# A forgetting attention inside a three-layer kernel: masked terms from GpSimd, outputs turned by transposes, second products in one PSUM bank

## The chip, the cores and the metric

The kernel runs on one core of a Trainium2 chip, as one program and one launch. The metric is the device time of an execution in microseconds (us). The core has five engines that each work through their own list of instructions in order and meet at semaphores: TensorE (PE; its weight loads are shown as PEld), VectorE (DVE), ScalarE (ACT), GpSimd (POOL) and SyncE (SP, which here issues the DMAs). Matmuls and transposes of PE write to PSUM, which has eight banks of 512 fp32 columns; DVE and ACT read it, and GpSimd does not touch it in this kernel.

## The reference, cut to what matters

The whole program is three layers: a first block with attention and experts, a second layer with "forgetting" attention, and a third with windowed attention. Only the forgetting attention is touched. Per head (16 heads of width 64, 1024 positions) it computes

```python
c = jnp.cumsum(log_f, axis=1)                       # one forgetting sum per position and head
logits = einsum('bqhd,bkhd->bhqk', q_block, k) * scale
logits = logits + c_q[..., :, None] - c_k[..., None, :]
logits = where(k_pos <= q_pos, logits, -inf)        # causal
p = softmax(logits)
out_block = einsum('bhqk,bkhd->bqhd', p, v)         # 8 blocks of 128 queries
```

The term of the query is the same along a row of the softmax and drops out; the kernel adds only the term of the key.

## The kernel before, in words

The instructions stand in the order in which the Python code emits them; semaphores between the engines are added for every true dependence. `phase_fox` runs 16 heads of 8 units, one unit for each block `qt` of 128 queries, in the order 7, 0, 6, 1, 5, 2, 4, 3 within a head (units 0 to 127 in all). A unit has n = (qt+1)*128 keys and passes four stages, each emitted while later units pass their earlier ones:

- **First products** (lines 2040, 2041): q times the two parts of k, in pieces of 512 columns, into banks 0 and 1 (even places in the order) or bank 2 (odd places). A third matmul of 128 columns (line 2042) adds the causal mask `cm` to the diagonal block. Then DVE (line 2047) subtracts the products from the forgetting row `c`, writes the result to SBUF and takes the minimum of each row.
- **Exponential** one unit later (line 2051, ACT).
- **Transposes** three units later (line 2066, PE, up to four blocks to a bank of `p_tr`: banks 4, 5, 6). `split` makes two parts of each: ACT copies the bank (line 341, the high part), DVE subtracts (line 342, the low part).
- **Second products** `pv_chunks` (lines 1993, 1994): v times both parts, for a pair of query blocks with the higher one called `top` (7, 1, 5, 3), 256 columns, in pieces of two key blocks that wait in the list `todo` and are emitted two to a unit ahead of the unit's first products. ACT copies the finished sum to `OT` (`acopy`, line 315).

The second products and the folds take their PSUM from one ring of two banks, 3 and 7 (`p_pv`). When a head is done, `fold_chunks` multiplies `OT` with a 128x64 matrix `fold` (line 2013, eight fp32 matmuls), which adds the two halves and turns the output at once; DVE divides by the row sums (line 2016, four instructions) and writes the outputs `og`.

`fox_load(h+1)` loads q, k and then `c` for the next head. The table `WO_FOX` puts work for the output weights beside chosen units: at units 119 to 122 GpSimd splits a quarter of a weight each time (lines 344 and 335 through `split`). GpSimd has no other work in this stage.

Of the kernel before, what the change touches and what calls it, by code (L numbers as in the profile page):

```python
# [124 lines left out]
def view(t, shape, dtype, o):  # L125
    n = math.prod(shape[1:])
    ap = t[:shape[0], o:o + n]
    if dtype is not t.dtype:
        ap = ap.bitcast(dtype)
    if len(shape) > 2:  # L130
        names = "abcd"[:len(shape) - 1]
        ap = ap.rearrange(f"p ({' '.join(names)}) -> p {' '.join(names)}", **dict(zip(names, shape[1:])))
    return ap
# [160 lines left out]
def three_layer_kernel(ctx: ExitStack, tc: tile.TileContext, I, out, stop=99, dbg=None):  # L294
    nc = tc.nc
    V, A, G, T, SP = (GUARD(e) for e in (nc.vector, nc.scalar, nc.gpsimd, nc.tensor, nc.sync))
    ctx.enter_context(tc.manual_schedule())
    sb = Arena(ctx.enter_context(tc.tile_pool(name="sbuf", bufs=1)), SLOTS, SMALL)
    banks = Banks(ctx.enter_context(tc.tile_pool(name="psum", bufs=1, space=PSUM)).tile([P, 4096], F32, name="ps"))
    p_mm = banks.ring([0], [1], [2], [3])  # L300
    p_s = banks.ring([0, 1], [2, 3])
    p_tr = banks.ring([4], [5], [6])
# [25 lines left out]
    def bc_load(dst, src_row, n):  # L328
        SP.dma_start(out=dst, in_=bass.AP(tensor=src_row.tensor, offset=src_row.offset,
                                          ap=[[0, dst.shape[0]], [1, n]]))  # L330
# [49 lines left out]
    def head_loads(dst, src, h, flip=False):  # L380

        for x in range(2):
            d, s = dst[x * 64:(x + 1) * 64], src[:, 1 - x if flip else x, h // 2]
            if len(dst.shape) == 2:
                SP.dma_start(out=f(d), in_=s[h % 2 * 64:(h % 2 + 1) * 64])
            else:
                SP.dma_start(out=f(d), in_=s.rearrange("(a p) n -> p a n", a=2))
# [1350 lines left out]
    FX = {}  # L1738

    def fox_load(h):  # L1740
        if h >= 16:
            return
        q = sb.tile([P, S], F32R, f"fq{h}")
        k = sb.tile([P, 2, S], F32R, f"fk{h}")
        c = sb.tile([P, S], F32, f"fc{h}")
        head_loads(q, d_aq, h)
        for x in range(2):
            head_loads(k[:, x], d_ak, h, x == 1)
        bc_load(c, d_c[h], S)
# [211 lines left out]

    def phase_fox(og, wo, last):

        p_s0, p_s1, p_pv = banks.ring([0, 1]), banks.ring([2]), banks.ring([3], [7])
        fc, pp, ptp, sm, ob = Rings(sb), Rings(sb, 2), Rings(sb, 2), Rings(sb, 4), Rings(sb, 2)
        cm, idr = fc.tile([P, P], F32R, name="cm"), fc.tile([P, P], F32R, name="idr")
        cmf = fc.tile([P, P], F32, name="cmf")
        V.memset(cmf, 0.0)
        G.affine_select(out=cmf, in_=cmf, compare_op=OP.is_ge, fill=-BIG, base=0, pattern=[[-1, P]],
                        channel_multiplier=1)  # L1970
        V.tensor_copy(cm, cmf)
        V.tensor_copy(idr, ident)
        fc.drop("cmf")
        pp.reserve_pairs("sb", 2)
        pp.reserve_pairs("pt", 4)
        OT, RS, PT = {}, {}, {}
        todo = Todo(FDELAY)


        ORDER = ((7, 0, 6, 1), (5, 2, 4, 3))  # L1980

        def pv_chunks(h, top, hi, lo):

            v = FX[h][3]
            box = {}

            def chunk(k0, k1):
                if k0 == 0:
                    box["ps"] = p_pv.tile([P, 256], name="pv")
                ps = box["ps"]  # L1990
                for kt in range(k0, k1):
                    q0 = P if kt == top else 0
                    T.matmul(ps[:, q0:], lhsT=v[:, kt], rhs=hi[:, kt, q0:], start=(kt == 0), stop=False)
                    T.matmul(ps[:, q0:], lhsT=v[:, kt], rhs=lo[:, kt, q0:], start=False, stop=(kt == top))
                if k1 == top + 1:
                    acopy(OT[h][:, (top - 1) * P:(top + 1) * P], ps)
                    if top == 3:
                        sb.drop(f"fv{h}")
                        fold_chunks(h)

            for k0 in range(0, top + 1, 2):
                todo.add(lambda k0=k0: chunk(k0, k0 + 2))

        def fold_chunks(h):
            box = {}

            def chunk(t0, t1):
                if t0 == 0:
                    box["po"] = p_pv.tile([P, NT, 64], name="po")
                    V.reciprocal(RS[h], RS[h])  # L2010
                po = box["po"]
                for t in range(t0, t1):
                    T.matmul(po[:, t], lhsT=OT[h][:, t * P:(t + 1) * P], rhs=fold, start=True, stop=True)
                if t1 == NT:
                    for t in range(0, NT, 2):
                        V.tensor_tensor(og[t // 2][:, :, h * 64:(h + 1) * 64], po[:, t:t + 2],
                                        RS[h][:, t:t + 2, None].to_broadcast([P, 2, 64]), op=OP.mult)

            for t0 in range(0, NT, 2):
                todo.add(lambda t0=t0: chunk(t0, t0 + 2))  # L2020

        def unit(h, half, i):
            todo.step()
            qt = ORDER[half][i]
            if half == 0 and i == 0:
                OT[h] = ob.tile([P, S], F32, name="ot", bufs=3)
                RS[h] = sm.tile([P, NT], F32, name="rs")
            if half == 0 and i == 3:
                fox_load(h + 1)
            if half == 1 and i == 2:  # L2030
                fox_load_v(h + 1)
            q, k, c = FX[h][:3]
            qs = slice(qt * P, (qt + 1) * P)
            n = (qt + 1) * P
            todo.some(FTAKE)
            ps = (p_s1 if i % 2 else p_s0).tile([P, 512 if i % 2 else S], name="s")
            for c0 in range(0, n, 512):
                w = min(512, n - c0)
                end = c0 + w == n
                T.matmul(ps[:, c0:c0 + w], lhsT=q[:, qs], rhs=k[:, 0, c0:c0 + w], start=True, stop=False)  # L2040
                T.matmul(ps[:, c0:c0 + w], lhsT=q[:, qs], rhs=k[:, 1, c0:c0 + w], start=False, stop=not end)
            T.matmul(ps[:, qs], lhsT=idr, rhs=cm, start=False, stop=True)  # L2042
            nm = sm.tile([P, 1], F32, name="nm")
            sbt = pp.tile([P, S], F32, name="sb")
            pt = pp.tile([P, S], F32, name="pt", bufs=4)

            V.tensor_tensor_reduce(sbt[:, :n], ps[:, :n], c[:, :n], -1.0, 3e38, OP.add, OP.min, nm)  # L2047
            if half == 1 and i == 3:
                sb.drop(f"fq{h}", f"fk{h}", f"fc{h}")
            yield  # L2050
            A.activation(out=pt[:, :n], in_=sbt[:, :n], func=AF.Exp, scale=-1.0, bias=nm,  # L2051
                         accum_out=RS[h][:, qt:qt + 1])
            yield
            yield
            kind = i % 2
            if i < 2:
                nb = (8, 4)[kind]
                PT[h, half, kind] = (ptp.tile([P, nb, 256], F32R, name=f"phi{kind}"),
                                     ptp.tile([P, nb, 256], F32R, name=f"plo{kind}"))
            hi, lo = PT[h, half, kind]  # L2060
            cs = slice((qt % 2) * P, (qt % 2 + 1) * P)
            for b in range(0, qt + 1, 4):
                m = min(4, qt + 1 - b)
                tr = p_tr.tile([P, 4, P], name="ptr")
                for j in range(m):
                    T.transpose(tr[:, j], pt[:, (b + j) * P:(b + j + 1) * P], ident)  # L2066
                split(hi[:, b:b + m, cs], lo[:, b:b + m, cs], tr[:, :m])
            if i >= 2:
                pv_chunks(h, qt | 1, hi, lo)

        for h in range(16):
            for half in range(2):
                for i in range(4):
                    wo.step(WO_FOX.get(8 * h + 4 * half + i, ()))
                    go.feed(unit(h, half, i))
        last()
        n = 0
        while go.active or go.fresh or not todo.empty():
            todo.step()
            todo.some(3)  # L2080
            go.feed()
            if n == 0:
                pp.drop("sb")
            if n == 2:
                pp.drop("pt")
            wo.step(WO_FOX.get(128 + n, ()))
            n += 1
        for r in (fc, pp, ptp, sm, ob):
            r.close()

    def new_og():
        return [sb.tile([P, 2, D], F32, f"og{q}") for q in range(4)]
# [294 lines left out]
```

## Time and profile before

| | |
|---|---|
| time, median of 3 runs | 2597.66 us (2596.23 to 2602.85) |
| the profiled execution | 2597.42 us, span 2595.7 us |
| share of the span, PE, PEld, DVE, ACT, POOL | 95%, 79%, 69%, 56%, 21% |
| the forgetting attention | about 1764.7 to 2016 us of the span |
| PE busy in 1780 to 1995 us | 214.78 of 215.00 us |

An engine's busy time counts its instructions from start to end; two that overlap count once. On PE the ends are modelled, so the distance from one start to the next says what an instruction costs there. In brackets behind an instruction stand its engine's idle time before it and the instruction that ended the wait.

### The profile page before, as it was taken

How to read it: one execution, taken by the hardware profiler on the slowest of the kernel's cores; microseconds unless marked ns; L12 is line 12 of the kernel's file. 1: busy time of each engine (PE TensorE's matmuls, PEld its weight loads, DVE VectorE, ACT ScalarE, POOL GpSimd, SP SyncE). 2: the span in 40 equal slices, each digit the busy share in tenths (PEclk: the TensorE clock that was granted, in tenths of full speed). 3: DMA queues.
4: the chain of work that ended last, by engine and by line, in shares of the span. 5: the costliest groups of instructions: out<-in, count | busy, mean ns of one | idle time of the engine just before them, and what ended most of it. 6: DMA issues, size and time to landing. Idle time of an engine off the chain costs nothing. (4 is left out here: it accounts for less than half of the span.)

```text
span 2595.7 us, 37353 instructions
## 1 busy us (share of the span) xinstructions
PE 2461.7 (95%) x13658; PEld 2053.3 (79%) x13658; DVE 1798.1 (69%) x3072; ACT 1458.0 (56%) x2557; POOL 557.7 (21%) x523
## 2 busy tenths in 40 slices
PE   5999899998988999999997999999999899999999
PEld 3789788887876777777765887899999789888977
DVE  7654588887668999999998354536888436735952
ACT  3324577777217878878874343436888224435930
POOL 0000089936002222222211012310002002300400
PEclk8999999999989999999998999999999899999999
DMA  7355765553748999999968524337667324338523
GB/s 267 114 140 164 231 195 162 172 185 110 255 162 307 384 390 386 385 380 382 381 245 315 166 89 147 112 111 198 165 171 204 114 85 147 118 110 190 148 73 106
DMA packets 270416, 530.04 MB, mean 204 GB/s; under 512 B 28027, under 2 KB 180603, under 8 KB 244118
## 3 DMA queue, kind: packets, MB, share of 16 engines
q1 hardware_dynamic: 263062, 510.84, 60.0%
q0 software_dynamic: 7168, 16.79, 1.9%
q8 instruction: 109, 1.79, 0.3%
q14 instruction: 77, 0.63, 0.1%
HBM read 424.19 MB, written 111.76 MB: 206 GB/s over the span
## 5 line engine op out<-in xcount | busy, mean ns | idle before, releaser
L365 PE MATMUL ps<-t,t 128*128 128x512 f32 (+5 forms) x8224 | 1758.3, 370 | 3.8 <-DVE t L342 2.4
L365 PEld LDWEIGHTS ps<-t,t 128*128 128x128 f32 (+1 forms) x8224 | 1377.0, 182 | 313.0 <-DVE t L342 4.4
L342 DVE TENSOR_TENSOR t<-t,t 128x2048 fp32r<-128x2048 f32 (+4 forms) x226 | 472.3, 2115 | 55.3 <-ACT t L341 55.2
L341 ACT ACTIVATE t<-ps 128x512 fp32r<-128x512 f32 (+3 forms) x660 | 334.2, 544 | 313.9 <-PE ps L377 205.1
L342 DVE TENSOR_TENSOR t<-ps,t 128x512 fp32r<-128x512 f32 (+3 forms) x660 | 391.8, 623 | 89.7 <-ACT t L341 83.2
L341 ACT ACTIVATE t<-t 128x2048 fp32r<-128x2048 f32 (+4 forms) x226 | 399.9, 1773 | 31.0 <-DVE t L774 10.9
L322 POOL TENSOR_TENSOR small<-small 128x8 f32<-128x8 f32 (+3 forms) x120 | 137.3, 1145 | 944.8 <-DVE small L321 912.2
L317 ACT ACTIVATE t<-ps,small 96x512 f32<-96x512 f32 (+5 forms) x208 | 128.6, 618 | 322.8 <-PE ps L365 278.0
L335 POOL TENSOR_TENSOR t<-t,t 128x256 f32<-128x256 f32 (+1 forms) x224 | 166.3, 774 | 27.1 <-DMA t<-in_b_ada_dram 23.3
L315 ACT ACTIVATE t<-ps 128x256 f32<-128x256 f32 (+4 forms) x196 | 88.4, 453 | 125.0 <-PE ps L365 69.9
L377 PE MATMUL ps<-small,t 96*128 96x96 f32 (+1 forms) x736 | 94.3, 267 | 47.4 <-DMA t<-d_ye 18.0
L1512 POOL DMA_INDIRECT d_ye<-t,small x32 | 45.2, 1413 | 435.7 <-ACT t L317 429.1
L377 PEld LDWEIGHTS ps<-small,t 96*128 96x128 f32 (+1 forms) x736 | 82.4, 145 | 68.1 <-DVE t L1880 18.5
L2129 DVE TENSOR_TENSOR t<-t,ps 128x512 f32<-128x512 f32 x32 | 22.0, 688 | 125.8 <-PE ps L365 125.8
L2047 DVE CUSTOM_DVE_ANT_0 t<-ps,t 128x1024 f32<-128x1024 f32 (+7 forms) x128 | 95.5, 747 | 19.5 <-PE ps L2042 17.6
L349 DVE SCALAR_TENSOR_TENSOR t<-t,small,t 128x512 fp32r<-128x512 f32 (+5 forms) x124 | 80.2, 692 | 35.7 <-ACT t L348 35.7
L2051 ACT ACTIVATE t<-t,small 128x1024 f32<-128x1024 f32 (+7 forms) x128 | 99.3, 776 | 7.7 <-DVE small L2047 5.4
L626 POOL TENSOR_SCALAR t<-t,small 128x1024 f32<-128x1024 f32 x32 | 92.6, 2894 | 31.9 <-DMA t<-in_w_ada_dram 31.9
L1508 POOL DMA_INDIRECT t<-d_h,small x32 | 89.0, 2781 | 37.5 <-DVE small L1216 28.0
L1090 PE MATMUL ps<-t,t 128*128 128x512 f32 x320 | 83.6, 408 | 8.1 <-ACT t L1136 7.6
L1709 DVE TENSOR_REDUCE small<-t 128x8 f32<-128x512 f32 (+1 forms) x56 | 36.2, 647 | 79.0 <-ACT t L1708 79.0
L2066 PE MATMUL ps<-small,t 128*128 128x128 f32 x576 | 86.2, 277 | 0.4 <-ACT t L2051 0.3
(296 smaller groups left out, 2966.9 us busy)
## 6 DMA issues: line engine op xcount, KB each, us to landing
t<-in_w_expert_gate_dram SPq DMA_DIRECT2D x64, 1024.0 KB, 11.6
t<-in_w_expert_up_dram SPq DMA_DIRECT2D x64, 1024.0 KB, 11.1
t<-in_w_expert_down_dram SPq DMA_DIRECT2D x64, 1024.0 KB, 10.5
t<-in_w_ada_dram SPq DMA_DIRECT2D x48, 512.0 KB, 5.2
t<-d_ak SPq DMA_DIRECT2D x64, 256.0 KB, 4.7
t<-in_w_in_a_dram SPq DMA_DIRECT2D x12, 1024.0 KB, 9.1
t<-in_x_dram SPq DMA_DIRECT2D x16, 512.0 KB, 5.4
t<-d_dk SPq DMA_DIRECT2D x16, 512.0 KB, 8.7
```

The source lines that it names most:

```text
L315: A.activation(out=dst, in_=src, func=AF.Copy)
L317: A.activation(out=dst, in_=src, func=AF.Copy, scale=scale)
L322: G.tensor_tensor(dst, dst, mhalf[:, :dst.shape[-1]], op=OP.pow)
L335: G.tensor_tensor(out[:, c:c + 256], a[:, c:c + 256], b[:, c:c + 256], op=op)
L341: A.activation(out=hi, in_=src, func=AF.Copy)
L342: e.tensor_tensor(lo, src, f(hi), op=OP.subtract)
L365: T.matmul(ps, lhsT=a(k), rhs=b(k), start=(first and i == 0), stop=(last and i == n - 1))
L377: T.transpose(ps[:, k], src[:, (c + k) * P:(c + k + 1) * P], ident[:m, :m])
L626: G.tensor_scalar(w, w, cc[:, k:k + 1], None, op0=OP.mult)
L1508: G.indirect_dma_start(out=xg[e % 3], out_offset=None, in_=d_h2, in_offset=rows(idx_in[:CAP, e:e + 1]), bounds_check=S - 1, oob_is_err=False)
L2047: V.tensor_tensor_reduce(sbt[:, :n], ps[:, :n], c[:, :n], -1.0, 3e38, OP.add, OP.min, nm)
L2051: A.activation(out=pt[:, :n], in_=sbt[:, :n], func=AF.Exp, scale=-1.0, bias=nm, accum_out=RS[h][:, qt:qt + 1])
```

## The change

The mask leaves PE: before a unit, GpSimd writes the forgetting row with a large negative number above the diagonal (`masked`, in place for the blocks 4 to 7, into a buffer `cs` for the blocks 0 to 3), two units ahead of the DVE instruction that reads it. The folds leave PE: four blocks of `OT` at a time are turned by plain transposes (`turn`), DVE adds the two halves (a `reduce_sum` of 512 elements out of PSUM), and GpSimd divides and writes `og`. The second products use the two halves of bank 7 in turn (`pv_half`), and bank 3 goes to the ring of the transposes. `c` is loaded ahead of q and k.

```diff
-        bc_load(c, d_c[h], S)                      # fox_load: c first, then q, k
+        bc_load(c, d_c[h], S)
...
-        p_s0, p_s1, p_pv = banks.ring([0, 1]), banks.ring([2]), banks.ring([3], [7])
+        p_s0, p_s1 = banks.ring([0, 1]), banks.ring([2])
+        p_tr.groups = [3], [4], [5], [6]
+        npv = [0]
+        def pv_half():
+            npv[0] += 1
+            return view(banks.t, [P, 256], F32, 7 * 512 + npv[0] % 2 * 256)
...
+        def masked(h, qt):
+            c = FX[h][2]
+            n = (qt + 1) * P
+            if qt > 3:
+                d = slice(qt * P, n)
+                G.affine_select(out=c[:, d], in_=c[:, d], compare_op=OP.is_ge, fill=-BIG, base=0, ...)
+                CS[qt] = c[:, :n]
+            else:
+                CS[qt] = cs[:, qt * (qt + 1) // 2 * P:][:, :n]
+                G.affine_select(out=CS[qt], in_=c[:, :n], compare_op=OP.is_ge, fill=-BIG, base=qt * P, ...)
...
-                    box["ps"] = p_pv.tile([P, 256], name="pv")
+                    box["ps"] = pv_half()
...
-                        fold_chunks(h)
+                    if top in (3, 5):
+                        todo.add(lambda: turn(h, 4 * (top == 5)))
...
+        def turn(h, t0):
+            V.reciprocal(RS[h][:, t0:t0 + 4], RS[h][:, t0:t0 + 4])
+            po = p_tr.tile([P, 4, P], name="po")
+            for t in range(4):
+                T.transpose(po[:, t], OT[h][:, (t0 + t) * P:(t0 + t + 1) * P], ident)
+            o = OT[h][:, t0 * P:t0 * P + 256].rearrange("p (t d) -> p t d", t=4)
+            V.reduce_sum(o, po.rearrange("p t (a d) -> p t d a", a=2), axis=AX.X)
+            for t in (0, 2):
+                G.tensor_tensor(og[(t0 + t) // 2][:, :, h * 64:(h + 1) * 64], o[:, t:t + 2],
+                                RS[h][:, t0 + t:t0 + t + 2, None].to_broadcast([P, 2, 64]), op=OP.mult)
...
-            T.matmul(ps[:, qs], lhsT=idr, rhs=cm, start=False, stop=True)
-            V.tensor_tensor_reduce(sbt[:, :n], ps[:, :n], c[:, :n], -1.0, 3e38, OP.add, OP.min, nm)
+            V.tensor_tensor_reduce(sbt[:, :n], ps[:, :n], CS[qt], -1.0, 3e38, OP.add, OP.min, nm)
+            u = 8 * h + 4 * half + i + 2
+            if u < 128:
+                masked(u // 8, ORDER[u // 4 % 2][u % 4])
```

In the changed kernel the first products stand in lines 2051 and 2052, the second in 2010 and 2011, the transposes in 2079, the exponential in 2064, the turn in 2027, its sum in 2029, its division in 2031, and the masks in 1983 (in place) and 1988 (into `cs`). Three places show what moves.

PE, in the middle of a head, where one second product ends and the next begins. Before (after the eight transposes of block 7, then `top` 1 and `top` 5):

```order
L1993 MATMUL ps<-t_13206,t_13046 128x256
L1994 MATMUL ps<-t_13207,t_13046 128x256
L1993 MATMUL ps<-t_13206,t_13046 128x128
L1994 MATMUL ps<-t_13207,t_13046 128x128
L1993 MATMUL ps<-t_13178,t_13046 128x256 [waits DVE_49]
L1994 MATMUL ps<-t_13180,t_13046 128x256
```

Now (the end of `top` 5, then `top` 3, behind the transpose of block 0):

```order
L2079 MATMUL ps<-small,t_13146 128x128
L2010 MATMUL ps<-t_13184,t_13216 128x256
L2011 MATMUL ps<-t_13186,t_13216 128x256
L2010 MATMUL ps<-t_13184,t_13216 128x128
L2011 MATMUL ps<-t_13186,t_13216 128x128
L2010 MATMUL ps<-t_13215,t_13216 128x256 [waits Activation_49]
L2011 MATMUL ps<-t_13216 128x256 [waits DVE_49]
```

The first matmul of each second product now has a wait on ACT's counter, and the count it waits for in the built program is the one that the `acopy` of the product just ahead of it raises: the wait is kept by bank, not by half.

ACT, in one head, from the exponential of block 7 on. Before:

```order
L2051 ACTIVATE t_13152,small<-t_13151,small 128x1024
L341 ACTIVATE t_13206<-ps 128x4x128
L2051 ACTIVATE t_13152,small<-t_13151,small 128x128
L341 ACTIVATE t_13177<-ps 128x4x128 x2
L2051 ACTIVATE t_13153,small<-t_13151,small 128x896
L315 ACTIVATE t_13156<-ps 128x256
L341 ACTIVATE t_13206<-ps 128x128
L2051 ACTIVATE t_13153,small<-t_13151,small 128x256
L315 ACTIVATE t_13156<-ps 128x256
```

Now:

```order
L2064 ACTIVATE t_13146,small<-t_13145,small 128x1024
L315 ACTIVATE t_13156<-ps 128x256
L341 ACTIVATE t_13215<-ps 128x4x128
L2064 ACTIVATE t_13146,small<-t_13145,small 128x128
L315 ACTIVATE t_13156<-ps 128x256
L341 ACTIVATE t_13183<-ps 128x4x128 x2
L2064 ACTIVATE t_13147,small<-t_13145,small 128x896
L341 ACTIVATE t_13200<-ps 128x128
L2064 ACTIVATE t_13147,small<-t_13145,small 128x256
L315 ACTIVATE t_13156<-ps 128x256
```

The copies (L315) of `top` 7 and of `top` 5 stand behind the exponentials of blocks 7 and 1, and PE's next second product is right behind each of them.

POOL, from the first split of output weights (L344, L335) of units 119 to 122 on, with the divisions (L2031) and masks (L1983, L1988) that now stand between; before, the splits stood one behind the other:

```order
L344 CAST t_15954<-t_13359 128x1024 [waits DMAHW3_49,DMAHW1_49,DMAHW6_49,DMAHW0_49,PE_49]
L335 TENSOR_TENSOR t_15955<-t_13359,t_15954 128x256 [waits DMAHW1_49,DMAHW0_49,DMAHW6_49,PE_49,Pool_49]
L335 TENSOR_TENSOR t_15955<-t_13359,t_15954 128x256 x3
L2031 TENSOR_TENSOR t_13142<-t_13156,small 128x2x64 [waits DVE_49,Activation_49]
L2031 TENSOR_TENSOR t_13143<-t_13156,small 128x2x64
L1988 AFFINE_SELECT t_13144<-t_15874 128x128
L344 CAST t_15954<-t_13157 128x1024 [waits DMAHW4_49]
L335 TENSOR_TENSOR t_15955<-t_13157,t_15954 128x256 [waits Pool_49]
L335 TENSOR_TENSOR t_15955<-t_13157,t_15954 128x256 x3
L1983 AFFINE_SELECT t_15874<-t_15874 128x128 [waits DVE_49]
L344 CAST t_16017<-t_15784 128x1024 [waits DMAHW5_49,DMAHW1_49,DMAHW6_49,DMAHW0_49,PE_49]
```

A split (one L344, four L335) now has a mask before it and the next mask behind it, up to the mask of unit 124.

## Rows read from the trace of the kernel before

**Rows 1.** Busy time by stretch: us, engines with counts, clock, DMA share, GB/s.
```profile
1780.00:1995.00 215.00, 214.78 (x1721) 206.79 (x1720) 176.16 (x457) 177.34 (x451) 9.47 (x13) 1.00 0.69 181
```
**Rows 2.** Waits in 1764.7 to 2016: us in total, times, longest.
```profile
ACT t L341 <- PE ps L2066: 36.1, 60, 1.2
```
**Rows 3.** The mask's matmul: duration ns min/median/max, first and last start.
```profile
L2042 PE MATMUL ps<-t x128: 221/224/308, 1765.7 to 2008.7; 128*128 128x128 f32 x128
```
**Rows 4.** Timeline of one head, PE: start us, us, engine, line.
```profile
1887.02 0.22 PE L2042 MATMUL ps<-t 128*128 128x128 f32 x1
1887.08 0.71 PE L2066 MATMUL ps<-small,t 128*128 128x128 f32 x5
1887.63 1.00 PE L2013 MATMUL ps<-small,t 128*128 128x64 f32 x8
...
1888.45 0.31 PE L2040 MATMUL ps<-t,t 128*128 128x128 f32 x1
...
1888.70 0.28 PE L2042 MATMUL ps<-t 128*128 128x128 f32 x1
...
1888.82 0.62 PE L2066 MATMUL ps<-small,t 128*128 128x128 f32 x4
...
1889.27 1.00 PE L2013 MATMUL ps<-small,t 128*128 128x64 f32 x8
...
1890.09 0.48 PE L2040 MATMUL ps<-t,t 128*128 128x512 f32 x1
...
1890.99 0.22 PE L2042 MATMUL ps<-t 128*128 128x128 f32 x1
1891.05 1.04 PE L2066 MATMUL ps<-small,t 128*128 128x128 f32 x8
...
1891.85 0.36 PE L1993 MATMUL ps<-t,t 128*128 128x256 f32 x1
...
1892.34 0.33 PE L1993 MATMUL ps<-t,t 128*128 128x256 f32 x1
...
1892.87 0.28 PE L2040 MATMUL ps<-t,t 128*128 128x256 f32 x1
...
1893.11 0.23 PE L2042 MATMUL ps<-t 128*128 128x128 f32 x1
```
**Rows 5.** Timeline of the same head, DVE and ACT.
```profile
1887.28 1.23 DVE L2047 CUSTOM_DVE_ANT_0 t<-ps,t 128x1024 f32<-128x1024 f32 x1 [0.84 <-PE ps L2042]
...
1888.61 1.15 ACT L2051 ACTIVATE t<-t,small 128x1024 f32<-128x1024 f32 x1
...
1891.69 1.09 ACT L341 ACTIVATE t<-ps 128x512 fp32r<-128x512 f32 x2 [0.97 <-PE ps L2066]
...
1892.95 1.05 ACT L2051 ACTIVATE t<-t,small 128x896 f32<-128x896 f32 x1 [0.18 <-DVE small L2047]
...
1894.00 0.36 ACT L315 ACTIVATE t<-ps 128x256 f32<-128x256 f32 x1
...
1894.26 0.26 ACT L341 ACTIVATE t<-ps 128x128 fp32r<-128x128 f32 x1
...
1894.49 0.51 ACT L2051 ACTIVATE t<-t,small 128x256 f32<-128x256 f32 x1
```
**Rows 6.** DVE by line and shape, a sum elsewhere: count, busy, mean ns.
```profile
L1709 DVE TENSOR_REDUCE small<-t 128x8 f32<-128x512 f32 x48 | 32.9, 686 | 76.2 <-ACT t L1708 76.2
```
**Rows 7.** Timeline of POOL: the mask once, and a split of output weights.
```profile
1763.60 0.29 POOL L1969 TENSOR_SCALAR_AFFINE_SELECT t<-t 128x128 f32<-128x128 f32 x1 [56.75 <-DVE t L1968]
1982.95 1.04 POOL L344 CAST t<-t 128x1024 fp32r<-128x1024 f32 x1 [219.06 <-PE ps L2013]
1984.07 2.83 POOL L335 TENSOR_TENSOR t<-t,t 128x256 fp32r<-128x256 f32 x4
```
**Rows 8.** Timeline of the stage's end.
```profile
2017.67 0.64 ACT L315 ACTIVATE t<-ps 128x256 f32<-128x256 f32 x2
2018.10 2.54 PE L2013 MATMUL ps<-small,t 128*128 128x64 f32 x16 [1.86 <-ACT t L315]
```

More of the change, by code (lines that the diff above doesn't have):

```diff
@@ L1962, in phase_fox @@
     def phase_fox(og, wo, last):
-        p_s0, p_s1, p_pv = banks.ring([0, 1]), banks.ring([2]), banks.ring([3], [7])
-        fc, pp, ptp, sm, ob = Rings(sb), Rings(sb, 2), Rings(sb, 2), Rings(sb, 4), Rings(sb, 2)
[L1966 to L1973, printed above, removed]
+        p_s0, p_s1 = banks.ring([0, 1]), banks.ring([2])
[4 more added lines that the diff above has]
+            return view(banks.t, [P, 256], F32, 7 * 512 + npv[0] % 2 * 256)
+        fc, pp, ptp, sm, ob = Rings(sb), Rings(sb, 2), Rings(sb, 2), Rings(sb, 4), Rings(sb, 2)
+        CS, cs = {}, fc.tile([P, 10 * P], F32, name="cs")
+        def masked(h, qt):
[3 more added lines that the diff above has]
+                d = slice(qt * P, n)
+                G.affine_select(out=c[:, d], in_=c[:, d], compare_op=OP.is_ge, fill=-BIG, base=0, pattern=[[-1, P]],
+                                channel_multiplier=1)
+                CS[qt] = c[:, :n]
+            else:
+                CS[qt] = cs[:, qt * (qt + 1) // 2 * P:][:, :n]
+                G.affine_select(out=CS[qt], in_=c[:, :n], compare_op=OP.is_ge, fill=-BIG, base=qt * P,
+                                pattern=[[-1, n]], channel_multiplier=1)
         pp.reserve_pairs("sb", 2)
@@ L1998, in chunk @@
                         sb.drop(f"fv{h}")
-                        fold_chunks(h)
+                    if top in (3, 5):
+                        todo.add(lambda: turn(h, 4 * (top == 5)))
             for k0 in range(0, top + 1, 2):
                 todo.add(lambda k0=k0: chunk(k0, k0 + 2))
[L2004 to L2020, printed above, removed]
+        def turn(h, t0):
[8 more added lines that the diff above has]
+                                RS[h][:, t0 + t:t0 + t + 2, None].to_broadcast([P, 2, 64]), op=OP.mult)
         def unit(h, half, i):
@@ L2038, in unit @@
                 w = min(512, n - c0)
-                end = c0 + w == n
                 T.matmul(ps[:, c0:c0 + w], lhsT=q[:, qs], rhs=k[:, 0, c0:c0 + w], start=True, stop=False)
-                T.matmul(ps[:, c0:c0 + w], lhsT=q[:, qs], rhs=k[:, 1, c0:c0 + w], start=False, stop=not end)
-            T.matmul(ps[:, qs], lhsT=idr, rhs=cm, start=False, stop=True)
+                T.matmul(ps[:, c0:c0 + w], lhsT=q[:, qs], rhs=k[:, 1, c0:c0 + w], start=False, stop=True)
             nm = sm.tile([P, 1], F32, name="nm")
@@ L2069, in unit @@
                 pv_chunks(h, qt | 1, hi, lo)
+        masked(0, 7)
+        masked(0, 0)
         for h in range(16):
@@ L2089, in phase_fox @@
             r.close()
+        p_tr.groups = [4], [5], [6]
     def new_og():
```

## The prediction

> **What bounds the kernel now.** I read the page first for the stage that the edit touches, then the busy time by stretch, the waits of that stage, and last the timeline of one head. From 1780 to 1995 us PE is busy for 214.78 of 215.00 us at full granted clock, while DVE is busy for 176.16 and ACT for 177.34 (82% each) [rows 1]. The waits agree: what is idle long is ACT, waiting for transposes, 36.1 us [rows 2]. So the stage goes at PE's pace, and its two helpers have 18% of slack. The mask's 128 matmuls, one for each unit, start from 1765.7 to 2008.7 us [rows 3]: 243.0/127 = 1.913 us for a unit, 15.3 us for a head of eight. PE's ends are modelled, so I cost it by the distance from one start to the next.
>
> **What PE loses.** A mask matmul takes 0.06 us (1887.02 to 1887.08, 1890.99 to 1891.05), and 0.12 where the piece ahead of it is only 128 wide (1888.70 to 1888.82) [rows 4]. That is six and two in a head: 0.60 us. The folds of a head take 1887.63 to 1888.45 and 1889.27 to 1890.09, 1.64 us; the eight transposes in their place cost what eight take in the same rows, 1891.05 to 1891.85, 0.80 us [rows 4]. Together PE is relieved of 0.60 + 1.64 - 0.80 = 1.44 us a head, 23.0 us in 16 heads. If nothing else changed, a head would take 13.9 us.
>
> **What the helpers get.** DVE loses four divisions and gets two sums of 512 elements out of PSUM. No row has that form; 512 elements summed in SBUF take 0.69 us [rows 6], and an instruction that reads 1024 elements from PSUM takes 1.23 [rows 5], so a sum costs between these, and I take the former, which has its count. DVE's busy time of 176.16/215.00 x 15.3 = 12.5 us a head [rows 1] and two sums make 13.9, less the four divisions that it loses: it fits under PE's 13.9, with little to spare. GpSimd's mask of 128 columns takes 0.29 us [rows 7]; up to 512 columns lie between that and the 1.04 of a cast over 1024 [rows 7], 0.6 by interpolation. Four of 0.29 and 0.3, 0.4, 0.5, 0.6 are 3.0 us a head. A division of 128 elements lies below the 2.83/4 = 0.71 of a 256-wide subtraction [rows 7]; I take 0.45, four a head. GpSimd's 4.8 us a head are far below a head's time, and a mask has two units, some 4 us, from the end of the DVE instruction that it must let pass to the one that needs it. So in the steady heads the masks hide beside DVE and PE. Loading c first delays q and k by one issue on SP's queue; they are loaded a head ahead, so I put that at nothing, up to 1 us before the last head, where the output weights are loaded too.
>
> **What PE gets: a wait.** Before, a second product began in a bank whose last reader was two products back. Now the first matmul of each of them waits until ACT has copied the one just ahead. ACT is in order, so PE then waits for all that stands before that copy on ACT, and whatever is behind the matmul on PE waits along: the rest of the second product, the next unit's first products, the next transposes, and through them DVE. Four such starts come in a head. Two have 1.6 us and more of PE work between (first products and six or eight transposes), and the copy is early on ACT; they cost nothing. The other two are these.
>
> Behind block 7. Count from the end of its first products, 1887.02 [rows 4]. DVE starts its minimum 0.26 later and the exponential comes 1888.61 - 1887.02 = 1.59 after; it runs 1.15 [rows 5], then the copy, 0.36 (the copy at 1894.00) [rows 5], and PE starts 0.07 after a copy's end (2017.67 + 0.36 to 2018.10) [rows 8]: 3.17 us. PE meanwhile has the five transposes of block 4 (0.55), the last piece of `top` 7 (0.49, as 1891.85 to 1892.34), a turn (0.40), the first products of block 0 (0.25) and four transposes (1888.82 to 1889.27, 0.45) [rows 4]: 2.14 us. The wait is 1.03 us.
>
> Behind block 6. Count from 1890.99, when the transposes of block 7 would start. The two copies of its transposes begin 0.64 after these (1891.05 to 1891.69) and last 1.09; then the exponential of 896 (1.05), a copy (0.23, 1894.26 to 1894.49), the exponential of 256 (0.51), the `acopy` of `top` 5 (0.36) and 0.07: 3.95 us [rows 4, 5, 8]. PE has eight transposes (0.80), eight matmuls of the second product (twice 1892.34 to 1892.87, 1.06), first products of block 1 (1892.87 to 1893.11, 0.24), one transpose (0.10) and the last piece (0.49) [rows 4]: 2.69 us. The wait is 1.26 us.
>
> Together 2.29 us a head; the first head has no earlier one to wait for, so 15 heads make 34.4 us. From both sides: if the chains are 0.4 shorter each, 22; if DVE, fuller now, is late by 0.5 in each, 49.
>
> The Trainium skill, "PSUM — Partial Sum Buffer", section "PSUM bank collisions raise a hardware error", says that two engines must be kept apart by bank and quadrant, not by address, which speaks against giving one bank to two products. No run here shows a collision; the waits in the changed program follow that rule. By it the second half of bank 7 is no second buffer, and the time is the forecast; were halves independent, it would be the first rival's.
>
> **The end of the stage.** Four splits of output weights at units 119 to 122 take 1.04 + 0.08 + 2.83 = 3.95 us each on GpSimd [rows 7]. Before, nothing stood beside them and they ran from 1982.95, though unit 119 is only at about 1765.7 + 119 x 1.913 = 1993 [rows 3, 7]: five units early. Now they stand between masks, and the mask of unit 118 waits for DVE at unit 116. From there to unit 124, which needs the last mask behind them, are eight units, 16.2 us at the new pace; GpSimd has seven masks (2.5), four splits (15.8) and four divisions (1.8): 20.1 us. DVE, and PE two units after it, are late by about 4 us; nothing late if the slack of the units' pipeline takes it, 7 if DMAs hold the first of them. At the very end, ACT's two copies came at 2017.67 behind the second weight's splits, and the folds at 2018.10 took 2.54 us [rows 8]. Now the last second product stands between the two copies, then copy, turn, sum and division: 1.0 + 0.43 + 0.8 + 0.7 + 0.45 = 3.4 us, against 2.54 for the folds; I add 1 us (0 to 2).
>
> **Sum**, against the profiled execution of 2597.42 us, which is the median of the runs (2597.66) to 0.3: 2597.4 - 23.0 + 34.4 + 4 + 1 = 2613.8; I say 2614 us, 0.6% slower. A head goes from 15.3 to about 16.2 us.
>
> **Rivals.**
> 1. PE's relief stays (the other side). ACT, with 18% of slack, comes to the copies earlier than I count, or the wait is not by bank in effect, so the two waits together are far under 1.44 us a head, the point from which it decides. Then PE's 23.0 us are won less the end's 5: 2579 us. For it: PE almost never waits now [rows 1]. Against: the exponentials that stand before the copies start from PE's own first products, so ACT can't be early. Chance 0.06.
> 2. The waits and the relief cancel: 1.1 to 1.7 us of waits a head, because the exponentials and copies overlap more when ACT has a queue. 15 x 1.4 = 21 us against 23, with the end's 5: about 2600, within 0.3% (2590 to 2605), which is about what a measurement of this kernel can tell from no change. Chance 0.12.
> 3. The helpers are late on top. With sums of 1.23 us DVE has up to 15.0 us a head, in order, and each wait of PE starts from its minimum; or GpSimd's masks, now one for each unit, take twice the 0.29. A further 1.3 us a head is 20 us: 2634. For it: DVE's fuller load; against: both have idle time in 16.2 us. Chance 0.12.
>
> The forecast has 0.70. Slower by over 0.3% is the forecast and the third, 0.82; within 0.3% 0.12; faster 0.06. The range, 2601 to 2632, takes in the forecast's own bounds (22 to 49 us of waits, 0 to 7 at the end) as far as they are likely together.
>
> **What would show it.** In the profile of the changed kernel PE waits for ACT at line 315 about twice a head, some 30 to 36 us in all, ahead of lines 2010 and its weight loads; lines 2042 and 2013 are gone, and PE is busy for less than 90% of the stage. DVE waits for POOL's masks once, for some us, around units 122 to 124, and hardly elsewhere. Wrong would be: no wait of PE for line 315, or a head under 15.3 us, or DVE waiting for masks in every head.

## The result

| | before | changed |
|---|---|---|
| median of the runs on one chip, us | 2600.10 | 2624.81 |
| lowest to highest, us | 2596.23 to 2602.85 | 2620.54 to 2627.52 |
| ratio to before, 95% interval | | 1.0093 (1.0078 to 1.0109) |
| profiled execution, us (span) | 2597.42 (2595.7) | 2627.16 (2625.1) |

The change makes the kernel 24.7 us slower by the medians. Forecast were 16.4 us more than the profiled execution, 2614 us in a range of 2601 to 2632. The side and the mechanism were right; the size was a third too small.

The two profiled executions lie 29.7 us apart, which is 5 us more than the medians. That part is older than the stage. Here is the last but one gate product on DVE, in code that the edit doesn't touch, of before and then of the changed kernel (start, length, engine, line, operation, and in brackets the idle time ahead with what ended it):

```profile
1747.03 0.52 DVE L1734 SCALAR_TENSOR_TENSOR t<-t,t 128x346 f32<-128x346 f32 x1 [3.28 <-ACT t L1732]
```

```profile
1751.58 0.52 DVE L1734 SCALAR_TENSOR_TENSOR t<-t,t 128x346 f32<-128x346 f32 x1 [3.28 <-ACT t L1732]
```

It stands 4.55 us later. In the profiled runs of the experiments below the stage's first minimum starts anywhere from 1766.2 to 1775.8 us, whatever the kernel does later; so this is scatter of an execution, and I count from the stage's first minimum on.

### The profile page after: what moved, and what is told of

Read it like the earlier page. It is cut to its first block, busy times and chain, and to the rows that moved or that the text cites. A ratio compares the mean times of both kernels' runs of the same rounds, so it can differ in the third digit from the quotient of the medians.

```text
span 2625.1 us, 37134 instructions
## 1 busy us (share of the span) xinstructions
PE 2451.1 (93%) x13402; PEld 2031.4 (77%) x13402; DVE 1803.9 (69%) x3053; ACT 1457.3 (56%) x2557; POOL 627.7 (24%) x714
## 5 line engine op out<-in xcount | busy, mean ns | idle before, releaser
L342 DVE TENSOR_TENSOR t<-t,t 128x2048 fp32r<-128x2048 f32 (+4 forms) x226 | 471.5, 2112 | 56.2 <-ACT t L341 56.0
L342 DVE TENSOR_TENSOR t<-ps,t 128x512 fp32r<-128x512 f32 (+3 forms) x660 | 392.0, 623 | 78.7 <-ACT t L341 77.6
L335 POOL TENSOR_TENSOR t<-t,t 128x256 f32<-128x256 f32 (+1 forms) x224 | 168.2, 784 | 26.7 <-DMA t<-in_b_ada_dram 22.8
L315 ACT ACTIVATE t<-ps 128x256 f32<-128x256 f32 (+4 forms) x196 | 89.0, 455 | 126.2 <-PE ps L365 69.1
L2010 PE MATMUL ps<-t,t 128*128 128x256 f32 x320 | 89.7, 306 | 37.6 <-ACT t L315 37.5
L2010 PEld LDWEIGHTS ps<-t,t 128*128 128x128 f32 x320 | 61.3, 192 | 43.5 <-ACT t L315 43.1
```

What stands on the lines that cost most here:

```text
L315: A.activation(out=dst, in_=src, func=AF.Copy)
L335: G.tensor_tensor(out[:, c:c + 256], a[:, c:c + 256], b[:, c:c + 256], op=op)
L342: e.tensor_tensor(lo, src, f(hi), op=OP.subtract)
```

## The profile after

**The stage.** The view of the minimum's line, of before and of the changed kernel (durations in ns, then first and last start), gives the stage's length:

```profile
L2047 DVE CUSTOM_DVE_ANT_0 t<-ps,t x128: 236/753/1225, 1767.1 to 2009.0; 128x1024 f32<-128x1024 f32 x16, 128x128 f32<-128x128 f32 x16, 128x896 f32<-128x896 f32 x16, 128x256 f32<-128x256 f32 x16
```

```profile
L2057 DVE CUSTOM_DVE_ANT_0 t<-ps,t x128: 279/748/1225, 1771.9 to 2038.3; 128x1024 f32<-128x1024 f32 x16, 128x128 f32<-128x128 f32 x16, 128x896 f32<-128x896 f32 x16, 128x256 f32<-128x256 f32 x16
```

From the first to the last of 128 units it is 241.9 us before and 266.5 now: 24.6 us more, which is the whole difference of the medians. Busy time in the stretch of [rows 1], with the same columns:

```profile
1780.00:1995.00 215.00, 185.01 (x1375) 169.43 (x1376) 164.72 (x408) 160.01 (x411) 52.54 (x149) 1.00 0.62 163
```

PE was busy for all of the stretch [rows 1] and is now for 86% of it, at full granted clock. What it waits for stands in the waits of the stage, 1764 to 2045 us (us in total, times, longest); before, no line of PE came to more than 2.1 us:

```profile
DVE t L2057 <- PE ps L2052: 42.3, 29, 2.4
PE ps L2010 <- ACT t L315: 35.0, 29, 3.0
DVE t L2057 <- POOL t L1988: 5.2, 15, 1.7
DVE t L2057 <- POOL t L1983: 3.5, 1, 3.5
PE ps L2052 <- DMA t<-d_ak: 1.5, 2, 1.2
```

The second line is the forecast wait: PE's first matmul of a second product (L2010) behind ACT's copy (L315), 35.0 us in 29 waits: none in head 0, one in head 1 (2.19 us), two in every later head. Line by line in one head, PE:

```profile
1887.29 0.27 PE L2079 MATMUL ps<-small,t 128*128 128x128 f32 x1
1888.52 0.39 PE L2010 MATMUL ps<-t,t 128*128 128x256 f32 x1 [0.96 <-ACT t L315]
...
1892.37 0.28 PE L2011 MATMUL ps<-t,t 128*128 128x128 f32 x1
1893.86 0.39 PE L2010 MATMUL ps<-t,t 128*128 128x256 f32 x1 [1.22 <-ACT t L315]
...
1898.44 0.60 PE L2027 MATMUL ps<-small,t 128*128 128x128 f32 x4
1898.79 0.37 PE L2010 MATMUL ps<-t,t 128*128 128x256 f32 x1
```

and ACT beside it:

```profile
1886.96 1.15 ACT L2064 ACTIVATE t<-t,small 128x1024 f32<-128x1024 f32 x1 [0.22 <-DVE small L2057]
...
1888.11 0.36 ACT L315 ACTIVATE t<-ps 128x256 f32<-128x256 f32 x1
...
1891.50 1.04 ACT L2064 ACTIVATE t<-t,small 128x896 f32<-128x896 f32 x1
...
1892.53 0.27 ACT L341 ACTIVATE t<-ps 128x128 fp32r<-128x128 f32 x1
1892.94 0.51 ACT L2064 ACTIVATE t<-t,small 128x256 f32<-128x256 f32 x1
...
1893.44 0.36 ACT L315 ACTIVATE t<-ps 128x256 f32<-128x256 f32 x1
```

Each copy comes right behind an exponential, and PE goes on 0.05 to 0.06 us after the copy's end. The idle time in brackets (0.96 and 1.22) starts at a modelled end. By starts the loss is larger: from 1887.29 to 1888.52 are 1.23 us, where the transpose of a single block is followed at 0.04 in before (1893.17 to 1893.21), 1.19 lost; from 1892.37 to 1893.86 are 1.49, where 0.11 is usual (1894.07 to 1894.18 in before), 1.38 lost. Together 2.57 us a head. The usual distances, in before:

```profile
1893.17 0.29 PE L2066 MATMUL ps<-small,t 128*128 128x128 f32 x1
1893.21 0.36 PE L1993 MATMUL ps<-t,t 128*128 128x256 f32 x1
...
1894.07 0.27 PE L1994 MATMUL ps<-t,t 128*128 128x128 f32 x1
1894.18 0.45 PE L2040 MATMUL ps<-t,t 128*128 128x512 f32 x1
```

A steady head, from one minimum of block 7 to the next (before: 1871.84, 1887.28, 1902.72, so 15.44 us):

```profile
1885.63 1.23 DVE L2057 CUSTOM_DVE_ANT_0 t<-ps,t 128x1024 f32<-128x1024 f32 x1 [0.20 <-POOL t L1988]
...
1887.67 0.66 DVE L2029 TENSOR_REDUCE t<-ps 128x256 f32<-128x512 f32 x1
...
1902.31 1.23 DVE L2057 CUSTOM_DVE_ANT_0 t<-ps,t 128x1024 f32<-128x1024 f32 x1 [0.20 <-POOL t L1988]
```

16.68 us. It is 1.24 us longer: 2.57 lost in waits, 1.33 won back by PE's shorter work. The distances between the 128 minima of both kernels, put in order of the heads, give the sum: heads 0 to 2 add 0.59, 2.01 and 1.47 us, heads 3 to 13 1.24 or 1.25 each (13.7), head 14 1.69, units 120 to 127 5.13; 24.6 in all, and the next stage starts 0.2 later still.

**The end.** GpSimd's splits now stand between masks (L1983, L1988), and DVE waits for the masks behind the last of them:

```profile
2028.60 1.03 POOL L344 CAST t<-t 128x1024 fp32r<-128x1024 f32 x1
2028.67 0.42 DVE L2057 CUSTOM_DVE_ANT_0 t<-ps,t 128x256 f32<-128x256 f32 x1 [1.74 <-POOL t L1988]
2029.71 2.80 POOL L335 TENSOR_TENSOR t<-t,t 128x256 fp32r<-128x256 f32 x4
2032.46 0.29 POOL L1983 TENSOR_SCALAR_AFFINE_SELECT t<-t 128x128 f32<-128x128 f32 x1
2032.71 0.51 POOL L1988 TENSOR_SCALAR_AFFINE_SELECT t<-t 128x384 f32<-128x384 f32 x1
2032.79 0.96 DVE L2057 CUSTOM_DVE_ANT_0 t<-ps,t 128x768 f32<-128x768 f32 x1 [3.48 <-POOL t L1983]
```

From unit 0 to unit 7 a steady head takes 2.13 us more than before; the last head takes 5.13 more, so masks behind splits cost 3.0 us.

**The start.** Head 1's k now comes one issue later, and PE waits for it once, in the first products of its block 7, at the end of head 0:

```profile
1783.26 0.44 PE L2051 MATMUL ps<-t,t 128*128 128x512 f32 x1
1784.87 0.47 PE L2052 MATMUL ps<-t,t 128*128 128x512 f32 x1 [1.17 <-DMA t<-d_ak]
```

1.61 us where 0.23 is usual: 1.4 us.

## The experiments

Each is given by its edit, the expectation written before it ran, and what it did. Medians are beside runs of the kernel before on the same chip (2600.3 to 2601.0 us). Line numbers move a little from kernel to kernel; the program's names don't. A steady head is 15.44 us before and 16.69 in the changed kernel. What a wait costs by starts is counted over heads 6 and 7, against the same places in kernels where nothing waits there.

**two_banks.** Undo the shared bank alone:

```
-        p_s0, p_s1 = banks.ring([0, 1]), banks.ring([2])
-        p_tr.groups = [3], [4], [5], [6]
+        p_s0, p_s1, p_pv = banks.ring([0, 1]), banks.ring([2]), banks.ring([3], [7])
...
-                    box["ps"] = pv_half()
+                    box["ps"] = p_pv.tile([P, 256], name="pv")
```

> The changed kernel with one thing put back: second products take whole banks 3 and 7 in turn, transposes the three banks 4 to 6. Theory A (the shared bank): the waits of PE for the copy of the product ahead, 2.5 us a head in 15 heads, about 37 us, go, and the relief of PE shows: 2580 to 2592 us, a head of 14.0 to 14.5 us against 16.69, and next to no wait of PE for line 315. Theory B (helpers: DVE with its sums, or GpSimd's masks, set the pace, and the wait at the bank only shows where the delay comes up): a head stays above 16 us, 2613 to 2627 us, and the wait turns up at the sums or at the minima instead.

2599.06 us, ratio 0.9997 (0.9986 to 1.0008). Busy time in the stage, the minima of two heads and the waits that concern banks:

```profile
1780.00:1995.00 215.00, 205.02 (x1531) 186.64 (x1530) 182.39 (x454) 178.00 (x455) 66.94 (x178) 1.00 0.70 185
```

```profile
1885.93 1.23 DVE L2049 CUSTOM_DVE_ANT_0 t<-ps,t 128x1024 f32<-128x1024 f32 x1 [0.56 <-POOL t L1980]
...
1900.93 1.23 DVE L2049 CUSTOM_DVE_ANT_0 t<-ps,t 128x1024 f32<-128x1024 f32 x1 [0.56 <-POOL t L1980]
```

```profile
PEld ps L2071 <- DVE t L342: 10.8, 28, 0.6
PEld ps L2019 <- DVE t L342: 5.2, 14, 0.4
```

The waits for L315 are gone and some 25 us with them: the shared bank is what makes the changed kernel slower. But the rest is worth nothing in sum, 7 us over A's range. A head takes 15.00 us, 0.44 less than before and not 1.0 to 1.4; the last head takes 17.68 us against 13.15, with three waits of DVE for POOL (1.9, 1.3 and 3.5 us). Theory A is right on the bank and wrong on the relief behind it. What is new in the list are weight loads of transposes (L2071) and of turns (L2019) that wait for DVE's splitting of an earlier transpose (L342): with three transposing banks a turn takes one that a transpose needs, three waits a head. By starts they cost PE 0.9 us a head.

**before_half.** Do the shared bank alone, in the kernel before:

```
-        p_s0, p_s1, p_pv = banks.ring([0, 1]), banks.ring([2]), banks.ring([3], [7])
+        p_s0, p_s1, p_po = banks.ring([0, 1]), banks.ring([2]), banks.ring([3])
...
-                    box["ps"] = p_pv.tile([P, 256], name="pv")
+                    box["ps"] = pv_half()
...
-                    box["po"] = p_pv.tile([P, NT, 64], name="po")
+                    box["po"] = p_po.tile([P, NT, 64], name="po")
```

> The kernel before with the bank change alone: second products in the two halves of bank 7, the folds keep bank 3, nothing else. Theory A: the same two waits, shorter because PE still has folds and mask matmuls between: behind block 7 1.03 - 0.42 (folds against a turn) - 0.12 (masks), behind block 6 1.26 - 0.12, and some 0.15 more each for the refilling of PE's pipeline, 1.9 us a head, 29 us in 15 heads: 2620 to 2636 us. Theory B: the bank by itself costs little, since ACT has slack: 2597 to 2606 us.

2638.26 us, ratio 1.0147 (1.0129 to 1.0165), just above A's range. The wait comes once a head and not twice, here from 1780 to 1995 us:

```profile
PE ps L2000 <- ACT t L315: 23.1, 12, 2.1
```

It stands behind the exponential of 896 elements: 2.07 us by starts, 17.54 us a head. The expectation had two waits of 0.6 and 1.3 us; that their sum of 1.9 comes so near is luck. (The 0.15 that it adds to each wait is what the forecast's waits fell short by; the part on the prediction explains it by PE's shorter work, and no refilling is needed.) That folds and masks cover the other wait is argued and not shown. Four of the heads take 19.1 us; of that more at the end.

**copy_dve.** The changed kernel, with the copy on DVE:

```
-                    acopy(OT[h][:, (top - 1) * P:(top + 1) * P], ps)
+                    V.tensor_copy(OT[h][:, (top - 1) * P:(top + 1) * P], ps)
```

> The changed kernel, halves of one bank kept, but the copy of a second product made by DVE and not by ACT. Theory A: what PE waits for is mainly the exponential that stands ahead of the copy on ACT; on DVE no exponential is ahead, so the waits fall from 2.2 to 0.5 to 1.2 us a head and the time to 2597 to 2614 us, though DVE gets some 1.6 us more a head. Theory B (DVE is the pace): slower than the changed kernel, 2630 to 2650 us.

2615.67 us, ratio 1.0064 (1.0046 to 1.0082): 9.1 us faster than the changed kernel, though DVE has four more instructions a head. A head takes 15.9 us, and PE's wait is

```profile
PE ps L2010 <- DVE t L2013: 19.1, 26, 1.5
```

in 215 us, 1.4 us a head against 2.2, more than the 0.5 to 1.2 expected. So part of the wait is the exponential ahead of the copy, and theory B, by which more work on DVE makes it slower, falls. What makes up the rest of the wait on DVE was not taken apart. The time is 1.7 us over A's range.

**late_splits.** The changed kernel, the four splits behind the last mask:

```
-WO_FOX = {112: [("load", 0)], 119: [("split", 0, (0,), 1)], 120: [("split", 0, (1,), 1)],
-          121: [("split", 0, (2,), 1)], 122: [("split", 0, (3,), 1)], 124: [("load", 1)],
+WO_FOX = {112: [("load", 0)], 124: [("load", 1)], 126: [("split", 0, (0,), 1)], 127: [("split", 0, (1,), 1)],
+          128: [("split", 0, (2,), 1)], 129: [("split", 0, (3,), 1)],
```

> The changed kernel with the four GpSimd splits of the first output weights at units 126 to 129, behind the last mask (unit 127's, issued at unit 125), in place of units 119 to 122. If the masks that stand behind splits cost what the minima of units 122 to 124 lose beyond other heads, 3.0 us: 2621 to 2623 us, and no wait of DVE for POOL over 0.3 us there. If the splits are late for the output product then, they give it back and more: up to 8 us later, 2633 us. Theory B has no view on it.

2631.26 us, ratio 1.0125 (1.0107 to 1.0143). The last head falls from 18.28 to 15.33 us, the 3.0 us that the masks cost; then the second weight's splits on ACT wait for the first's:

```profile
2044.26 3.90 ACT L341 ACTIVATE t<-t 128x1024 fp32r<-128x1024 f32 x4 [9.90 <-POOL t L335]
```

The second branch of the expectation: given back, and more.

**turn_in_pv.** two_banks, with the turns in the second products' banks:

```
-            po = p_tr.tile([P, 4, P], name="po")
+            po = p_pv.tile([P, 4, P], name="po")
```

> As two_banks, and the turned outputs go through the second products' two banks, as the folds did, and no longer through the three transposing banks. Open is why two_banks, free of the shared bank, has a head of 15.00 us and not 14.0. Theory C (transposing banks): a turn holds one of three of them until DVE's sum, so transposes wait; freed of that a head is 14.0 to 14.6 us and the time 2583 to 2593 us. Theory D (masks: DVE's minimum of block 7 waits 0.56 us in each head for a GpSimd mask, and the rest is DVE's order): a head stays at 14.9 to 15.1 us, 2596 to 2602 us.

2603.92 us, ratio 1.0007 (0.9997 to 1.0017), neither theory. The waits of transposes are gone; in their place PE waits once a head for L315 again (12.8 us in 13 waits): a turn between two products shifts the order of two banks, so that the next product meets the one just ahead. A head takes 15.28 us.

**only_turns** and **only_masks** take the two halves of the change apart, in the kernel before with its banks:

```
-                        fold_chunks(h)
+                    if top in (3, 5):
+                        todo.add(lambda: turn(h, 4 * (top == 5)))
```

> The kernel before with the turns alone (through the three transposing banks, with DVE's sums and GpSimd's divisions); the mask stays a matmul, second products keep banks 3 and 7. PE is relieved of 1.64 - 0.80 = 0.84 us a head. Theory C: transposes wait for the bank that a turn holds, so a head is 15.2 to 15.5 us against 15.44, 2594 to 2602 us. Theory D: without masks on GpSimd nothing eats it: a head of 14.6 us, 2584 to 2590 us.

2601.33 us, ratio 0.9999 (0.9989 to 1.0008), 15.23 us a head: 0.21 won of 0.84. The waits of its stage have, once a head each,

```profile
PEld ps L2010 <- DVE t L342: 4.7, 13, 0.4
PEld ps L2061 <- DVE t L342: 4.6, 13, 0.4
```

a turn that waits for a transposing bank, and a transpose that waits for one. By starts PE loses 0.37 us a head ahead of these transposes and 0.27 ahead of the turn: 0.64, the whole of what is missing of 0.84. Theory C.

```
-            T.matmul(ps[:, qs], lhsT=idr, rhs=cm, start=False, stop=True)
...
-            V.tensor_tensor_reduce(sbt[:, :n], ps[:, :n], c[:, :n], -1.0, 3e38, OP.add, OP.min, nm)
+            V.tensor_tensor_reduce(sbt[:, :n], ps[:, :n], CS[qt], -1.0, 3e38, OP.add, OP.min, nm)
+            u = 8 * h + 4 * half + i + 2
+            if u < 128:
+                masked(u // 8, ORDER[u // 4 % 2][u % 4])
```

> The kernel before with GpSimd's masks alone (c loaded first); the folds stay, second products keep banks 3 and 7. PE is relieved of 0.60 us a head. Theory C: it gets most of that, a head of 14.8 to 15.0 us, 7 us in all, and loses 5 at the end, where splits stand between masks: 2595 to 2601 us. Theory D: the masks' wait eats the relief, a head of 15.3 to 15.5 us: 2601 to 2608 us.

2594.64 us, ratio 0.9979 (0.9965 to 0.9993), 0.4 us under C's range; 14.79 us a head: 0.65 won, against 0.60 by the mask's matmuls. Theory D falls: masks on GpSimd take nothing back in the steady heads. The last head takes 16.11 us against 13.15, and the same minimum as in the changed kernel waits for the same mask:

```profile
2001.23 0.96 DVE L2054 CUSTOM_DVE_ANT_0 t<-ps,t 128x768 f32<-128x768 f32 x1 [3.47 <-POOL t L1975]
```

**best1**: turn_in_pv, with masks issued earlier and splits in halves.

```
-            u = 8 * h + 4 * half + i + 2
-            if u < 128:
-                masked(u // 8, ORDER[u // 4 % 2][u % 4])
+            for ahead, blocks in ((2, (6, 5, 4)), (3, (7,)), (4, (0, 1, 2, 3))):
+                u = 8 * h + 4 * half + i + ahead
+                if u < 128 and ORDER[u // 4 % 2][u % 4] in blocks:
+                    masked(u // 8, ORDER[u // 4 % 2][u % 4])
```

> As turn_in_pv, and masks are issued earlier where nothing forbids it (block 7's three units ahead, those of blocks 0 to 3 four), and the four splits of output weights are cut in halves at units 110, 112, 114, 116, 120, 121, 123 and 124. Theory C: a head as in turn_in_pv or 0.2 less, and the 5 us that the last two heads lose come down to 1 or 2: 2577 to 2588 us. Theory D: the gain comes here and not in turn_in_pv: 2583 to 2590 us. If splits or divisions still stand before masks, DVE waits for POOL by over 1 us in units 116 to 126.

2600.43 us, ratio 0.9997 (0.9987 to 1.0006), over both ranges. The head stays at 15.28 us, the last falls to 13.90; but head 13 takes 17.59, where PE waits 1.62 us for k: the load of the weights, now at unit 106, stands ahead of head 14's loads.

**one_ring.** The changed kernel, all of banks 3 to 7 in one ring:

```
-        p_tr.groups = [3], [4], [5], [6]
+        p_tr.groups = [3], [4], [5], [6], [7]
...
-                    box["ps"] = pv_half()
+                    box["ps"] = p_tr.tile([P, 256], name="pv")
```

> The changed kernel, but transposes, second products and turns draw from one ring of five banks, 3 to 7, so that each comes back to a bank five tiles later. Theory C (it is banks that eat the relief: the shared bank in the changed kernel, the bank that a turn holds in two_banks, the ring's order in turn_in_pv): no waits of PE for line 315 nor of transposes for DVE over 3 us in the stage, a head of 14.0 to 14.6 us, and with the 5 us that the end loses 2583 to 2593 us. Theory D (DVE, fuller by its sums and waiting for masks): 14.9 to 15.2 us, 2596 to 2602 us.

2610.21 us, ratio 1.0035 (1.0022 to 1.0048); both missed. A head takes 15.64 us, and now it is a transpose that waits for a product's copy:

```profile
PE ps L2072 <- ACT t L315: 18.9, 13, 1.7
```

A product holds its bank much longer than a transpose does, and in one ring the transposes behind it wait for it. Still banks, but more of them in the ring was no remedy.

**best2** (one_ring with early masks and halved splits at units 114 to 124):

> As one_ring, with the early masks of best1 and the splits in halves at units 114, 115, 116, 118, 120, 121, 122 and 124, their load at unit 112 again (in best1 it stood ahead of the last heads' k). Theory C: a head as in one_ring, and the end loses 0 to 2 us in place of 5: 2579 to 2590 us. Theory D: 2592 to 2598 us, the end alone.

2611.37 us, ratio 1.0044 (1.0030 to 1.0057), over both ranges. **masks_best** (only_masks with the same two edits):

> As only_masks, with the early masks and the halved splits of best2. A head stays at 14.8 us, and what only_masks loses in its last head, 16.11 against 13.15 us, comes down to 0 to 1: 2589 to 2593 us by theory C and D alike. If the splits still delay masks: 2594 to 2597 us.

2599.73 us, ratio 0.9992 (0.9982 to 1.0001), again over both. Both have a head 14 of 21 to 23 us. In masks_best the wait of SP's queue, then GpSimd's half split, the issue of head 15's first load, and PE's first products of head 15 are:

```profile
SPq L330 <- POOL t L336: 7.2, 1, 7.2
```

```profile
1981.18 1.43 POOL L336 TENSOR_TENSOR t<-t,t 128x256 fp32r<-128x256 f32 x2
...
1982.64 0.34 SPq L330 DMA_DIRECT2D t<-d_c  x1
...
1992.05 0.77 PE L2057 MATMUL ps<-t,t 128*128 128x512 f32 x1 [3.78 <-DMA t<-d_ak]
```

The load waits for the half split and is issued when that ends (1981.18 + 1.43 = 1982.61, and 1982.64); in only_masks, whose stage starts at the same time to 0.01 us, it is issued at 1973.50, right behind the weights' load. So k comes late. Why the load has to wait for a split I read as memory: pieces split earlier take what head 15 was loaded into, and its loads get what the half split frees; the times fit, and no run tried it apart. Behind these waits the granted clock of masks_best is at 0.50 from 1990.3 to 2003.8 us, into the middle of its last head, which takes 16.37 us though DVE waits for no mask there: what halved splits are worth at the end can't be read from this run.

**masks_alt.** only_masks with the early masks and whole splits at every other unit:

```
+WO_FOX = {112: [("load", 0)], 119: [("split", 0, (0,), 1)], 121: [("split", 0, (1,), 1)],
+          123: [("split", 0, (2,), 1)], 125: [("split", 0, (3,), 1), ("load", 1)],
```

> As only_masks, with the early masks, and the four whole splits at units 119, 121, 123 and 125, so that a split always stands behind a mask whose minimum is two units off, and none waits for weights that have not landed. If the order on GpSimd is all that only_masks loses at its end: no wait of DVE for POOL over 0.5 us, a last head of 13.2 to 13.8 us against 16.11, 2589 to 2593 us. If the second half's load, now a unit later, holds the output product: 2594 to 2597 us.

2591.15 us, ratio 0.9963 (0.9951 to 0.9976): faster than both kernels, some 34 us ahead of the changed one. What the expectation says of weights that had not landed was a misreading of masks_best, as its rows above show; with splits no earlier than unit 119 head 15's loads are not held. No wait of DVE for POOL is left in the stage; the last head takes 12.65 us. PE is again what bounds it:

```profile
1780.00:1995.00 215.00, 212.84 (x1661) 201.92 (x1661) 179.94 (x473) 180.07 (x464) 43.67 (x120) 1.00 0.72 190
```

## Why the prediction was right, and where its size failed

**The two waits: right in place, number and cause; each 0.1 to 0.2 us too small.** Forecast 30 waits of 34.4 us in all, found 29 of 35.0 by the idle time; one behind the exponential of 1024, one behind those of 896 and 256 elements. two_banks takes them away and the loss with them; copy_dve shortens what stands ahead of the copy and the loss with it. The forecast went by starts, 1.03 and 1.26 us, so it is 1.19 and 1.38 that answer it: 0.28 us a head more. Both chains to the end of the copy were right, 3.17 and 3.95 us forecast, 3.18 (1885.34 to 1888.52) and 3.97 (1889.89 to 1893.86) found. Too large was the work that PE has meanwhile, 2.14 and 2.69 us: it takes 1.99 and 2.59. The five transposes take 0.46 and not 0.55, the four 0.40 and not 0.45, the single one 0.03 and not 0.10.

**PE's relief: 1.44 forecast, 1.33 found** in the changed kernel's steady heads (2.57 - 1.24). By starts masks and folds give what was forecast (0.59 and 0.89), but the second products' matmuls take 0.24 us a head more. The two errors together turn the forecast 0.85 us a head into 1.24. Over heads 3 to 13 that is 13.7 us in place of 9.4, the largest part of what was missing.

**The first heads: the step "the first head has no earlier one to wait for", with the relief counted in 16 heads, failed.** It gave -1.44 for head 0 and 0.85 each for the next two, 0.3 us; measured 4.1. Before, heads 0 and 1 take 13.5 and 14.1 us, not 15.4, because they hold no fold: the first stands at 1795.00, in head 2. So there are only masks to win there, while head 1 gets a turn and a wait of 2.19 us; PE sets the pace of that head before all the same (busy for 14.02 of 14.05 us). By unit 7 of head 0 0.8 us are won, some of it perhaps by the clock, which stands at 0.50 for 3.4 us in that head of before and not in the changed one.

**"Loading c first ... I put that at nothing" failed** by 1.4 us, once, for head 1's k, which is part of these 4.1. That wait of head 1 is in only_masks too, which loads c first (1.16 us), and not in the first heads of before, before_half and only_turns, which load it last.

**GpSimd and DVE: right.** A sum out of PSUM takes 0.66 us (0.69 taken), masks of 128 and 384 columns 0.29 and 0.51. DVE does wait for a mask in every head, which was to be a sign of being wrong, but for 0.20 us, and it costs next to nothing: the minimum of block 7 starts 0.29 us behind its first products (1885.34 to 1885.63), 0.26 forecast.

**The end: 5 forecast, 7.0 - 2.5 = 4.5 found.** Head 14 and units 120 to 127 add 1.69 + 5.13 and the step to the next stage 0.2; two steady heads would be 2.5. For the 3.0 us in units 120 to 127 late_splits and masks_alt show that it is the order on GpSimd; what head 14 loses beyond a steady head, 0.45, was not taken apart.

**The sum:** 9.4 + 0.3 + 1.7 (heads 14 and 15) + 5 = 16.4 forecast; 13.7 + 4.1 + 2.5 + 4.5 = 24.8 found.

**The rivals.** "PE's relief stays" was the one that I priced wrong: I gave it 2579 us if the waits were gone. They are gone in two_banks, and it takes 2599. The relief of the folds was not to be had in any of the four cuts of the banks that were tried: the turn has to sit in a bank, and each time something then waits for one (15.00 us a head with turns among three transposing banks, 15.28 in the products', 15.64 in one ring, 16.69 with a fourth transposing bank and one for the products). That the bank is the cause is shown for each by the wait that is named. Counted by starts these waits cost 0.9, 1.2, 1.6 and 2.6 us a head, and without them each head would take 14.1: the relief is there, and the wait takes it back. Turns with a bank to themselves, and products guarded by half and not by bank, were not tried. "The helpers are late on top" did not happen in the steady heads.

## What to carry to other kernels

Where a program guards PSUM by bank, as this one does, two results in the halves of one bank are one buffer and not two: price such a change by what stands ahead of the reader on its engine, and look where the bank that it frees is spent. When work moves from an engine to another, ask not only for time there but for the bank or slot that it now sits in, and for what else stands in that engine's order; here masks alone were worth 0.65 us a head, and turns alone 0.21 of the 0.84 that they relieve PE of. A stage's first heads don't hold all the work of a steady head, so a gain per head isn't multiplied by all heads.

## What was not expected of the hardware

In before_half PE idles for 1.9 us in each head, and in four of 14 heads the granted clock falls behind that wait. Two heads beside each other, and the microseconds in the second (us, engines with counts, clock, DMA share, GB/s):

```profile
1816.77:1834.30 17.53, 15.63 (x126) 14.95 (x125) 12.75 (x33) 12.81 (x32) 0.00 (x0) 1.00 0.59 151
1834.30:1853.40 19.10, 17.20 (x126) 16.42 (x125) 12.70 (x34) 12.88 (x32) 0.00 (x0) 0.91 0.54 138
```

```profile
1842.00:1843.00 1.00, 1.00 (x10) 1.00 (x9) 0.49 (x3) 0.28 (x1) 0.00 (x0) 0.80 0.08 16
1843.00:1844.00 1.00, 1.00 (x7) 1.00 (x7) 0.23 (x1) 0.60 (x2) 0.00 (x0) 0.50 0.00 0
...
1846.00:1847.00 1.00, 1.00 (x11) 1.00 (x10) 0.61 (x3) 0.66 (x2) 0.00 (x0) 0.99 0.00 0
```

```profile
1841.43 0.39 PE L2000 MATMUL ps<-t,t 128*128 128x256 f32 x1 [1.90 <-ACT t L315]
```

PE waited until 1841.43; at 1842.6 the clock goes to the lower level, 0.50 (1.2 of 2.4 GHz), for 3.4 us, though PE is busy then. In the other three heads it falls 0.3 to 1.6 us after the same wait has ended. Each such head costs 1.56 us more, 6.2 in all, without which before_half would lie inside its expected range. In the changed kernel, whose waits are 1.0 and 1.2 us, the clock stays at 1.00 in the steady heads; behind its one wait of 3.0 us, in the last head (until 2030.12), it is at 0.50 from 2031.6. So here a wait could cost more than its length; that the wait is what lowers the clock is read from the order of the two alone, and why one head in three or four is hit and the others with the same wait not is open.
